# FFN 1 of a hybrid encoder layer: two more feature tiles in the seven-product scheme, with the residual's load, the norm factor, the single tiles' SwiGLU and the bias spread put elsewhere

## The chip, the cores and the metric

The kernel runs on one core of a Trainium2 chip. The metric is the device time of one execution in microseconds; of a group of runs the median counts. The profile is one execution taken by the hardware profiler. It names the engines PE (matrix multiply), PEld (its weight loads), DVE (vector), ACT (activation), POOL (GpSimd) and SP, whose queue issues most transfers. A DMA issue of an engine's queue carries a q (SPq, ACTq).

## The reference

One layer of a streaming encoder for 512 tokens of width 1024, all in float32. The part in question is the first feed-forward block:

```python
def rms_norm(x, g):
    y = x * rsqrt(mean(x * x, axis=-1, keepdims=True) + 1e-6)
    return y * g

def swiglu(x, w1, w3, w2):
    return (silu(x @ w1) * (x @ w3)) @ w2

f = swiglu(rms_norm(h, ffn1_pre_g), ffn1_w1, ffn1_w3, ffn1_w2)   # D_FF = 2816
h = h + 0.5 * rms_norm(f, ffn1_post_g)
```

Behind it come the mixer (a recurrent branch, windowed attention with a relative-position bias and sinks, gates) and a second feed-forward block of the same shape. The change touches neither; only the table of the attention's bias is prepared during FFN 1.

## The kernel before, in words

**Numbers.** A float32 factor is split into a high and a low half (`hi`, `lo`, type float32r): ACT copies the value to `hi`, DVE subtracts `hi` from the value to get `lo` (`split2`, L191 and L192; for weights of single tiles `split_to`, L156 and L157). A product is three matmuls: hi·hi, lo·hi, hi·lo.

**Tiles.** The 2816 hidden features are 22 feature tiles of 128. Tile i of `w1a` is a weight tile [128, 1024], and so is tile i of `w3a`. A *single* tile is computed by a *unit* (`unit`, `mm_feat`, L201 to L203): 8 slices of 128 channels by 3 matmuls with 512 tokens, 24 matmuls into one bank of PSUM. The transposed input stands in `uT` (high and low half).

**Pairs.** From tile NC1 on, two tiles are computed together (`Pairs`): the product of a 2x2 block of weights (two tiles by two halves of the channels) with a 2x2 block of inputs (two halves of the channels by two halves of the tokens) takes seven block products in place of eight, with sums of weight blocks (S12, S34) and of input blocks (`t1` to `t4`). A *job* is one such pair of `w1a` or of `w3a`; jobs alternate (w1a pair, w3a pair, next w1a pair), and `f` of a job is its first tile. A block product is 12 matmuls with 256 tokens (`mm_s`, L473 to L475). The products of one job, in order, by weights and inputs: a11·b11 (bank bu), s1·t1 (bank bx), [the seventh product of the job before, a22·t4], s2·t2 (added to bu), a12·b21 (bank bc), s4·b22 (added to bx), s3·t3 (added to bu). Between them ACT copies bank contents out: L551 (bu behind the first product), L554 (bx behind s1), L560 (bu behind s2), L578 (bu behind s3). A product that adds to a bank must wait until ACT has copied what stood there. DVE forms the four result blocks (L569, L574, L579), and in a `w3a` job multiplies them with the `w1a` ones (L584, L585, L598). ACT's Silu of a `w1a` job is L593 to L595 and comes behind its seventh product, in the next job.

`prep(m, i)` prepares the weights of job m: step 0 forms S12 and S34 (L518 to L521, four sums of 512 columns, on POOL or on the engine handed over), step 1 splits the first raw tile (a11, a12), step 2 splits S12 (s1, s2), step 3 S34 (s3, s4), step 4 a22 (`w22`). Inside job n stand prep(n+1, 1) to (n+1, 4), prep(n+2, 0), and the loads of job n+3 (`raws`).

**Input blocks.** `xn` is the normalized input, x·g·R: 16 operations on DVE (`norm_x`, L773), which need the spread norm factor `Rb`. The blocks b11 (from `xn`) and t1, t2 are split into slots of their own (`to_slots`: Xh, Xl); b21, b22, t3, t4 are split into `uT`, once no single unit reads it any more (`to_uT`). `sums` forms t1 to t4 by three differences on DVE (L752 to L754) and one on POOL (L751).

**Norm factor.** The residual x is loaded token-major (`h_load`, four tiles h). ACT squares and sums each (L680); `rstd4` makes 1/rms with its root on ACT (L248); DVE puts it on four diagonals (`dgs`, L686); PE multiplies these with ones (L700, bank r), which spreads the factor over all partitions; ACT copies the bank to `Rb` (L701). The single units run on x·g without the factor; it is multiplied in afterwards (`silu_mul`, L433 and L434, then Silu L435 and the product L436).

**Bias.** The relative bias comes from a small matmul of a one-hot table with the bias table (`oh`, L691), a copy (`erow`, L693) and a transfer from POOL's queue to a scratch in memory (L696), which attention reads much later.

**Order.** Every engine works off its queue strictly in the order in which the program issues. `later(n, f)` puts the issue of f at the n-th following `point`; a point stands behind every four channel slices of a unit (two a unit) and behind every block product. Buffers of [128, 1024] are 42 slots that go round: a transfer or an operation that gets a slot waits until its last user is done. SP's queue loads weight tiles in the order of `order` (`dma_to`), by need and slot. The first three units (w1a 0, w3a 0, w1a 1) run channel slice by channel slice behind the first loads; nine matmuls on zeros ahead of them warm PE up.

The part of the run in question stands in this order on PE: the first three units, unit w3a 1, the bias matmul, the factor, eight single units (w1a 2 to w3a 5), the first pair job (w1a 6 and 7).

## Time and profile before

| | |
|---|---|
| time of the runs | median 1135.27 us of 3 (1135.0 to 1135.29) |
| profiled execution | 1135.67 us, its span 1133.8 us |
| busy, share of the span | PE 99%, PEld 89%, DVE 70%, ACT 52%, POOL 31% |
| granted clock | 0.998 |
| DMA | 124.94 MB, mean 110 GB/s |

The busy time of PE counts matmuls whose ends are modelled, so a busy PE is not PE at its peak. A timeline line gives start, length, engine, line of the code, operation, output<-inputs, shapes and count; in brackets stands how long the engine was idle before it, and what ended that. A line of the waits gives engine and line, whom they waited for, us in total, times, and the longest. A line of the stretches gives from:to, its length, then for PE, PEld, DVE, ACT and POOL the busy time and the number of instructions, then the clock, the DMA share and GB/s. A line of the DMA issues gives the number, the size and the median us from issue to landing.

### The profile page before, as it was taken

To read this page: it belongs to the slowest core of one execution; us is meant where nothing else is said; L and a number is where in the kernel's file an instruction comes from. 1 tells how busy PE (TensorE), PEld (TensorE's weight loads), DVE (VectorE), ACT (ScalarE), POOL (GpSimd) and SP (SyncE) were. 2 spreads that over 40 slices of the span, in tenths; PEclk is the share of its full clock that TensorE was granted. 3 is DMA by queue.
4 is the path that set the end of the run, shared out by engine and by line. 5 is a ranking of instruction groups with operands and counts; after the bars stand their busy time and mean duration, and the time that the engine had idled before them with its cause. 6 is when DMAs were issued, how large, how long until landed. Compare 5 with 4: busy or idle time off the path is not lost.

```text
span 1133.8 us, 17339 instructions
## 1 busy us (share of the span) xinstructions
PE 1125.3 (99%) x6763; PEld 1003.5 (89%) x6763; DVE 790.1 (70%) x1181; ACT 585.2 (52%) x1042; POOL 353.8 (31%) x265
## 2 busy tenths in 40 slices
PE   9999999999999999999999999999999999999997
PEld 7889999988889987888888888889999999998886
DVE  5997889885436747695678865767899777975313
ACT  6445555574324349844655663356555555574211
POOL 0148678500000000001555643000965566700000
PEclk9999999999999999999999999999999999999999
DMA  9953223264313311234122333531323332255101
GB/s 343 157 135 112 93 95 112 76 222 151 110 56 135 144 56 57 75 95 148 56 78 90 93 95 112 185 111 38 113 94 94 112 112 76 94 197 172 40 19 56
DMA packets 36945, 124.94 MB, mean 110 GB/s; under 512 B 4416, under 2 KB 6208, under 8 KB 36864
## 3 DMA queue, kind: packets, MB, share of 16 engines
q1 hardware_dynamic: 34272, 115.15, 30.3%
q0 software_dynamic: 2448, 8.43, 4.0%
q8 instruction: 53, 0.87, 0.3%
q10 hardware_dynamic: 144, 0.26, 0.1%
q14 instruction: 28, 0.23, 0.1%
HBM read 116.50 MB, written 7.33 MB: 109 GB/s over the span
## 4 chain that ended last, share of the span: by engine, by line
PE 93%; DVE 3%; ACT 2%; issue 1%; DMA 0%; SPq 0%; DVEq 0%
PE c L475 11%; PE c L474 11%; PE c L473 11%; PE f L202 10%; PE f L201 10%; PE f L203 10%; PE acc L220 8%; PE acc L221 8%; PE acc L219 8%; PE pt L1067 1%; PE s L1031 1%; PE s L1030 1%; PE tr L310 1%; PE o L1083 1%; PE o L1084 1%
## 5 line engine op out<-in xcount | busy, mean ns | idle before, releaser
L201 PE MATMUL f<-uT,whi 128*128 128x512 f32 (+1 forms) x504 | 184.2, 365 | 0.0
L202 PE MATMUL f<-uT,wlo 128*128 128x512 f32 (+1 forms) x504 | 183.0, 363 | 0.4 <-DVE wlo L157 0.3
L203 PE MATMUL f<-uT,whi 128*128 128x512 f32 (+1 forms) x504 | 182.6, 362 | 0.0
L219 PE MATMUL acc<-whi,hT 128*128 128x512 f32 x352 | 137.1, 390 | 0.0
L220 PE MATMUL acc<-wlo,hT 128*128 128x512 f32 x352 | 137.0, 389 | 0.0
L221 PE MATMUL acc<-whi,hT 128*128 128x512 f32 x352 | 136.9, 389 | 0.0
L474 PE MATMUL c<-Xh,wlo 128*128 128x256 f32 x432 | 122.3, 283 | 0.0
L475 PE MATMUL c<-Xl,whi 128*128 128x256 f32 x432 | 122.3, 283 | 0.0
L473 PE MATMUL c<-uT,whi 128*128 128x256 f32 x432 | 122.3, 283 | 0.0
L474 PE MATMUL c<-uT,wlo 128*128 128x256 f32 x432 | 122.3, 283 | 0.0
L475 PE MATMUL c<-uT,whi 128*128 128x256 f32 x432 | 122.3, 283 | 0.0
L473 PE MATMUL c<-Xh,whi 128*128 128x256 f32 x432 | 122.3, 283 | 0.0
L192 DVE TENSOR_TENSOR wlo<-S,whi 128x1024 fp32r<-128x1024 f32 x72 | 118.2, 1642 | 3.6 <-ACT whi L191 3.2
L202 PEld LDWEIGHTS f<-uT,wlo 128*128 128x128 f32 x504 | 95.2, 189 | 15.8 <-DVE wlo L157 1.6
L201 PEld LDWEIGHTS f<-uT,whi 128*128 128x128 f32 x504 | 95.1, 189 | 15.8 <-issue 1.4
L203 PEld LDWEIGHTS f<-uT,whi 128*128 128x128 f32 x504 | 95.1, 189 | 14.8
L473 PEld LDWEIGHTS c<-Xh,whi 128*128 128x128 f32 x432 | 82.9, 192 | 0.0
L474 PEld LDWEIGHTS c<-Xh,wlo 128*128 128x128 f32 x432 | 82.9, 192 | 0.0
L473 PEld LDWEIGHTS c<-uT,whi 128*128 128x128 f32 x432 | 82.9, 192 | 0.0
L474 PEld LDWEIGHTS c<-uT,wlo 128*128 128x128 f32 x432 | 82.9, 192 | 0.0
L475 PEld LDWEIGHTS c<-uT,whi 128*128 128x128 f32 x432 | 82.9, 192 | 0.0
L475 PEld LDWEIGHTS c<-Xl,whi 128*128 128x128 f32 x432 | 82.9, 192 | 0.0
(309 smaller groups left out, 2703.8 us busy)
## 6 DMA issues: line engine op xcount, KB each, us to landing
raw_w2a<-in_w2a_dram SPq DMA_DIRECT2D x22, 512.0 KB, 3.7
raw_w1b<-in_w1b_dram SPq DMA_DIRECT2D x22, 512.0 KB, 4.2
raw_w3b<-in_w3b_dram SPq DMA_DIRECT2D x22, 512.0 KB, 4.2
raw_w2b<-in_w2b_dram SPq DMA_DIRECT2D x22, 512.0 KB, 4.1
raw_w3a<-in_w3a_dram SPq DMA_DIRECT2D x21, 512.0 KB, 4.5
raw_w1a<-in_w1a_dram SPq DMA_DIRECT2D x20, 512.0 KB, 4.5
raw_wg<-in_wg_dram SPq DMA_DIRECT2D x16, 512.0 KB, 3.7
raw_xr<-in_xr_dram SPq DMA_DIRECT2D x8, 512.0 KB, 4.7
```

Source lines behind the costliest of these rows:

```text
L192: dve.tensor_tensor(out=lo, in0=src, in1=f32(hi), op=ALU.subtract)
L201: pe.matmul(ps[:, c0:c1], wh[:, s], h_, start=k == 0, stop=False)
L202: pe.matmul(ps[:, c0:c1], wl[:, s], h_, start=False, stop=False)
L203: pe.matmul(ps[:, c0:c1], wh[:, s], l_, start=False, stop=k == KT - 1)
L219: pe.matmul(acc[n], x[:, 0, c], wh[:, s], start=first, stop=False)
L220: pe.matmul(acc[n], x[:, 0, c], wl[:, s], start=False, stop=False)
L221: pe.matmul(acc[n], x[:, 1, c], wh[:, s], start=False, stop=last)
L310: pe.transpose(ps[:, k * P : (k + 1) * P], hg[:, kk * P : (kk + 1) * P], ident)
L473: pe.matmul(ps, wh[:, s], xh, start=first, stop=False, skip_group_check=True)
L474: pe.matmul(ps, wl[:, s], xh, start=False, stop=False, skip_group_check=True)
L475: pe.matmul(ps, wh[:, s], xl, start=False, stop=k == 3, skip_group_check=True)
L1030: pe.matmul(o, lq, KS[g][:, 0, k0 : k0 + n], start=True, stop=False)
```

## The change

NC1 goes from 6 to 4: tiles 4 and 5 are computed as a pair (two jobs) and no longer as four units. With that, the surrounding work is placed anew.

- The four residual tiles are loaded ahead of the third next weight tile (w1a 2) instead of behind it, and only w3a 1 is split ahead of the squares.
- The factor's matmuls and the copy to `Rb` are issued in the middle of unit w3a 1 (`later(1, factor)`) instead of behind it.
- The banks of the eight single units are copied out raw by ACT (`keep`, two to a slot). Their SwiGLU (`swiglu_late`: two multiplies by `Rb` on DVE, Silu on ACT, a multiply on DVE) runs in jobs 1 to 4, one tile each, behind the first product. `hid.f` has its first four places reserved for them.
- `norm_x`, the differences (`t_sums`) and the splits of b11, t1, t2 are spread over the points of five units instead of nine; the first preparation of job 0 comes behind them (its sums on DVE, as before), and of job 1 only step 0 is issued ahead.
- The load of Silu's activation table (a Silu of `tiny`) moves from behind the root to behind the last bank copy, ahead of b21's split.
- The bias tables are loaded in job 3 and spread in job 5.

```diff
@@ the first loads
-    dma_to(NS + 2)
+    dma_to(NS + 1)
     h_load([a["x"][t * P : (t + 1) * P, :] for t in range(NT)])
+    dma_to(NS + 2)
     hid, X1 = Hidden(), {}
+    hid.f += [None] * NC1
...
     dma_one(pairs_a.k0 + 1)
+    dma_to(NS + 4)
...
-    oh = slot([N_BUCKETS, NREL + 1 + N_HEADS], name="oh")
-    pool.dma_start(out=oh[:, : NREL + 1], in_=a["onehot"])
-    pool.dma_start(out=oh[:, NREL + 1 :], in_=a["rel_bias"])
@@ behind the first three units
-    split_to(NS + 2)
+    split_to(NS + 1)
...
-    r, q = rstd4(s4)
-    act.activation(tiny, q, AF.Silu)
+    r, _ = rstd4(s4)
...
-    pairs_a.prep(0, 0, dve)
-    ps.append(unit("w3a", 1))
-    pse = bank("e")
-    pe.matmul(pse[:N_HEADS, : NREL + 1], oh[:, NREL + 1 :], oh[:, : NREL + 1], start=True, stop=True)
...
-    act.activation(Rb, psr, AF.Copy)
-    pairs_a.prep(0, 1)
-    hid.f += [silu_mul(ps[0], ps[1], Rb), silu_mul(ps[2], ps[3], Rb)]
-    pairs_a.prep(0, 2)
-    later(1, lambda: pairs_a.prep(0, 3))
-    later(2, lambda: pairs_a.prep(0, 4))
+    def factor():
+        psr = bank("r")
+        for t in range(NT):
+            pe.matmul(psr[:, t * P : (t + 1) * P], ones, dgs[:, t, :], start=True, stop=True)
+        act.activation(Rb, psr, AF.Copy)
+    later(1, factor)
+    def bias_in():
+        oh.append(slot([N_BUCKETS, NREL + 1 + N_HEADS], name="oh"))
+        pool.dma_start(out=oh[0][:, : NREL + 1], in_=a["onehot"])
+        pool.dma_start(out=oh[0][:, NREL + 1 :], in_=a["rel_bias"])
+    def bias_spread():
+        pse = bank("e")
+        t = oh.pop()
+        pe.matmul(pse[:N_HEADS, : NREL + 1], t[:, NREL + 1 :], t[:, : NREL + 1], start=True, stop=True)
+        erow = slot([N_HEADS, NREL + 1], name="erow")
+        act.activation(erow, pse[:N_HEADS, : NREL + 1], AF.Copy)
...
@@ the single units and the input blocks
-    def swiglu_units(na, nb, f0, f1, hid, R=None):
-        for f in range(f0, f1):
-            p1, p3 = unit(na, f), unit(nb, f)
-            later(1, lambda p1=p1, p3=p3: hid.f.append(silu_mul(p1, p3, R)))
+    def keep(f, e, ps):
+        if f not in raw:
+            raw[f] = slot([P, 2, SEQ], name="raw")
+        act.activation(raw[f][:, e, :], ps, AF.Copy)
+    def swiglu_late(f):
+        t = raw.pop(f)
+        for e in range(2):
+            dve.tensor_tensor(out=t[:, e, :], in0=t[:, e, :], in1=Rb, op=ALU.mult)
+        act.activation(t[:, 0, :], t[:, 0, :], AF.Silu)
+        dve.tensor_tensor(out=t[:, 1, :], in0=t[:, 1, :], in1=t[:, 0, :], op=ALU.mult)
+        hid.f[f] = t[:, 1, :]
+    def single(nm, i, ahead):
+        w = get(nm, i, ahead=ahead)
+        ps = bank("f")
+        mm_feat(ps, w)
+        return ps
...
-    for k in range(KT):
-        later(2 + k // 2, lambda k=k: norm_x(k))
-    later(6, lambda: xts.clear())
-    later(6, lambda: tn.extend(sums(xn)))
-    later(7, lambda: X1.update(b11=to_slots(xn[0, 0])))
-    later(9, lambda: X1.update(t1=to_slots(tn[0])))
-    later(11, lambda: X1.update(t2=to_slots(tn[1])))
-    end = 2 * 2 * (NC1 - 2)
-    for i, at_ in enumerate((end - 5, end - 2, end - 1)):
-        later(at_, lambda i=i: pairs_a.prep(1, i))
-    swiglu_units("w1a", "w3a", 2, NC1, hid, Rb)
+    def t_sums(n):
+        t = slot([P, 4, 256], name="T")
+        tn[n] = t
+        if n == 2:
+            pool.tensor_tensor(out=t, in0=xn[1, 1], in1=xn[0, 1], op=ALU.subtract)
+            return
+        p, q = ((xn[0, 1], xn[0, 0]), (xn[1, 1], tn.get(0)), None, (xn[1, 0], tn.get(1)))[n]
+        dve.tensor_tensor(out=t, in0=p, in1=q, op=ALU.subtract)
+    for k in range(4):
+        later(1, lambda k=k: norm_x(k))
+    later(3, lambda: X1.update(b11=to_slots(xn[0, 0])))
+    later(3, lambda: t_sums(0))
+    for k in range(4, KT):
+        later(3 + (k > 5), lambda k=k: norm_x(k))
+    later(4, lambda: xts.clear())
+    later(5, lambda: X1.update(t1=to_slots(tn[0])))
+    later(5, lambda: t_sums(1))
+    later(6, lambda: t_sums(2))
+    later(6, lambda: t_sums(3))
+    later(6, lambda: X1.update(t2=to_slots(tn[1])))
+    later(7, lambda: pairs_a.prep(0, 0, dve))
+    later(7, lambda: pairs_a.prep(0, 1))
+    later(8, lambda: pairs_a.prep(0, 2))
+    later(9, lambda: pairs_a.prep(0, 3))
+    later(10, lambda: pairs_a.prep(1, 0))
+    later(10, lambda: pairs_a.prep(0, 4))
+    later(7, lambda: dma_to(pairs_a.k0 + 4))
+    ps.append(single("w3a", 1, 1))
+    for n, p_ in enumerate(ps):
+        keep(n // 2, n % 2, p_)
+    p1 = single("w1a", 2, 1)
+    later(1, lambda: keep(2, 0, p1))
+    p3 = single("w3a", 2, 1)
+    later(1, lambda: keep(2, 1, p3))
+    p1_ = single("w1a", 3, 1)
+    later(1, lambda: keep(3, 0, p1_))
+    p3_ = single("w3a", 3, 0)
     point(True)
+    keep(3, 1, p3_)
+    act.activation(tiny, tiny, AF.Silu)
     X1["b21"] = to_uT(xn[1, 0], 1, 0)
     late = {
...
+        (3, 1): [bias_in],
+        (5, 3): [bias_spread],
     }
+    for f in range(NC1):
+        late.setdefault((f + 1, 1), []).append(lambda f=f: swiglu_late(f))
...
-NC1 = 6
+NC1 = 4
```

Job numbers count from the first pair job of the kernel in hand: job 0 is w1a 6 and 7 before, w1a 4 and 5 after.

More of the change, by code (lines that the diff above doesn't have):

```diff
@@ L639, in hybrid_layer @@
         load_x(2 * kp + 1)
+    dma_to(NS + 1)
+    h_load([a["x"][t * P : (t + 1) * P, :] for t in range(NT)])
     dma_to(NS + 2)
-    h_load([a["x"][t * P : (t + 1) * P, :] for t in range(NT)])
     hid, X1 = Hidden(), {}
+    hid.f += [None] * NC1
     pairs_a = Pairs("w1a", "w3a", NC1, X1, hid)
@@ L686, in hybrid_layer @@
         dve.tensor_scalar(out=dgs[:, t, :], in0=ident, scalar1=r[:, t : t + 1], scalar2=NEWT, op0=ALU.mult, op1=ALU.mult)
-    pairs_a.prep(0, 0, dve)
-    ps.append(unit("w3a", 1))
-    pse = bank("e")
-    pe.matmul(pse[:N_HEADS, : NREL + 1], oh[:, NREL + 1 :], oh[:, : NREL + 1], start=True, stop=True)
-    erow = slot([N_HEADS, NREL + 1], name="erow")
-    act.activation(erow, pse[:N_HEADS, : NREL + 1], AF.Copy)
-    scr = tc.dram_tile([N_HEADS, P, NREL], F32, name="bias_scr")
-    ev = erow[:, :NREL]
-    pool.dma_start(out=scr, in_=bass.AP(tensor=ev.tensor, offset=ev.offset, ap=[ev.ap[0], [0, P], ev.ap[1]]))
-    Rb = slot([P, SEQ], name="Rb")
-    psr = bank("r")
-    for t in range(NT):
-        pe.matmul(psr[:, t * P : (t + 1) * P], ones, dgs[:, t, :], start=True, stop=True)
-    act.activation(Rb, psr, AF.Copy)
-    pairs_a.prep(0, 1)
-    hid.f += [silu_mul(ps[0], ps[1], Rb), silu_mul(ps[2], ps[3], Rb)]
-    pairs_a.prep(0, 2)
-    later(1, lambda: pairs_a.prep(0, 3))
-    later(2, lambda: pairs_a.prep(0, 4))
+    Rb = slot([P, SEQ], name="Rb")
+    def factor():
[4 more added lines that the diff above has]
+    later(1, factor)
+    scr = tc.dram_tile([N_HEADS, P, NREL], F32, name="bias_scr")
+    oh = []
+    def bias_in():
[8 more added lines that the diff above has]
+        act.activation(erow, pse[:N_HEADS, : NREL + 1], AF.Copy)
+        ev = erow[:, :NREL]
+        pool.dma_start(out=scr, in_=bass.AP(tensor=ev.tensor, offset=ev.offset, ap=[ev.ap[0], [0, P], ev.ap[1]]))
     def softplus():
@@ L734, in softplus @@
                     scalar1=0.5, scalar2=None, op0=ALU.mult)
-    def swiglu_units(na, nb, f0, f1, hid, R=None):
-        for f in range(f0, f1):
-            p1, p3 = unit(na, f), unit(nb, f)
-            later(1, lambda p1=p1, p3=p3: hid.f.append(silu_mul(p1, p3, R)))
+    raw = {}
+    def keep(f, e, ps):
[14 more added lines that the diff above has]
+        return ps
     def uview(hh, th):
@@ L746, in pair_view @@
         return lambda e, k: p[e][:, k, :]
-    def sums(xf):
-        t = [slot([P, 4, 256], name="T") for _ in range(4)]
-        pool.tensor_tensor(out=t[2], in0=xf[1, 1], in1=xf[0, 1], op=ALU.subtract)
-        dve.tensor_tensor(out=t[0], in0=xf[0, 1], in1=xf[0, 0], op=ALU.subtract)
-        dve.tensor_tensor(out=t[1], in0=xf[1, 1], in1=t[0], op=ALU.subtract)
-        dve.tensor_tensor(out=t[3], in0=xf[1, 0], in1=t[1], op=ALU.subtract)
-        return t
     def to_slots(src):
@@ L765, in to_uT @@
         return uview(hh, th)
-    xn, tn = {(hh, th): slot([P, 4, 256], name="xn") for hh in range(2) for th in range(2)}, []
+    xn, tn = {(hh, th): slot([P, 4, 256], name="xn") for hh in range(2) for th in range(2)}, {}
     def norm_x(k):
```

## The prediction

> **What bounds the kernel now.** I read the page's totals and its chain first, then the waits of PE for the whole run, then the timelines of PE, DVE, POOL and ACT from the start to the second pair job.

> ```profile
> span 1133.8 us, 17339 instructions
> PE 1125.3 (99%) x6763; PEld 1003.5 (89%) x6763; DVE 790.1 (70%) x1181; ACT 585.2 (52%) x1042; POOL 353.8 (31%) x265
> PE 93%; DVE 3%; ACT 2%; issue 1%; DMA 0%; SPq 0%; DVEq 0%
> PE f L202 <- DVE wlo L157: 0.3, 1, 0.3
> ```

> PE is never let go: the last line is its longest wait behind the start. So the change wins exactly the PE work it removes, and loses every time something comes late. All it moves lies ahead of the sixth pair job. There the order of work is this (start, length):

> ```profile
> 22.71 0.39 PE L201 MATMUL f<-uT,whi 128*128 128x512 f32 x1
> 27.92 0.39 PE L203 MATMUL f<-uT,whi 128*128 128x512 f32 x1
> 28.98 1.16 PE L700 MATMUL r<-dgs,ones 128*128 128x128 f32 x8
> 29.90 0.48 PE L201 MATMUL f<-uT,whi 128*128 128x512 f32 x1
> 57.22 0.39 PE L201 MATMUL f<-uT,whi 128*128 128x512 f32 x1
> 57.90 0.50 PE L202 MATMUL f<-uT,wlo 128*128 128x512 f32 x1 [0.30 <-DVE wlo L157]
> 74.13 0.28 PE L473 MATMUL c<-Xh,whi 128*128 128x256 f32 x1
> 84.40 0.38 ACT L551 ACTIVATE ct<-c 128x256 f32<-128x256 f32 x1 [0.54 <-PE c L475]
> 94.48 0.39 ACT L551 ACTIVATE ct<-c 128x256 f32<-128x256 f32 x1 [0.53 <-PE c L475]
> 30.00:74.10 44.10, 43.80 (x194) 35.95 (x193) 41.40 (x52) 18.47 (x23) 10.75 (x6) 1.00 0.78 125
> ```

> The first two lines are matmuls 1 and 24 of unit w3a1: 5.21 us over 23 steps, 0.2265 us each, 5.44 a unit. ACT's copy L551 comes once a job: 10.08 us. The last line is the stretch of eight single units: of 44.1 us PE is busy 43.8 and DVE 41.4. DVE is nearly full there, and the change shortens this very stretch.

> **What decides: DVE and POOL block each other.** POOL's rows, then DVE's:

> ```profile
> 50.10 2.40 POOL L751 TENSOR_TENSOR T<-xn,xn 128x1024 f32<-128x1024 f32 x1 [18.73 <-DVE xn L773]
> 67.63 1.62 POOL L519 TENSOR_TENSOR S<-S,raw_w3a 128x512 f32<-128x512 f32 x1
> 69.32 2.16 POOL L520 TENSOR_TENSOR S<-raw_w3a,S 128x512 f32<-128x512 f32 x1
> 71.44 2.27 POOL L521 TENSOR_TENSOR S<-raw_w3a,raw_w3a 128x512 f32<-128x512 f32 x1
> 50.45 0.70 DVE L434 TENSOR_TENSOR sw<-f,Rb 128x512 f32<-128x512 f32 x1
> 51.25 1.81 DVE L436 TENSOR_TENSOR sw<-sw 128x512 f32<-128x512 f32 x1
> 56.63 1.22 DVE L157 TENSOR_TENSOR wlo<-raw_w3a,whi 128x1024 fp32r<-128x1024 f32 x1
> 68.17 2.16 DVE L192 TENSOR_TENSOR wlo<-raw_w3a,whi 128x1024 fp32r<-128x1024 f32 x1
> 70.37 2.19 DVE L192 TENSOR_TENSOR wlo<-S,whi 128x1024 fp32r<-128x1024 f32 x1
> ```

> The ends interlock: POOL 69.25, DVE 70.33, POOL 71.48, DVE 72.56, POOL 73.71. They take strict turns, 1.08 us for a 1024-wide DVE split, 1.15 for a 512-wide POOL sum; alone the split is 1.22, and 1.13 from one to the next where they follow each other. L436 ends at 53.06, 0.56 behind POOL's 52.50. L434, with one input from PSUM, was not slowed. So each POOL sum costs a waiting DVE queue its whole length.

> **The change, part by part.**

> *Tiles 4 and 5 paired.* Four units go, 4 x 5.44 = 21.74; two jobs come, 20.16: −1.6 us. The late wait at 57.9 goes: 57.90−57.22−0.23 = −0.45. The factor matmuls and the bias matmul stay on PE, elsewhere. Without any new wait −2.0.

> *Residual ahead.* SP now loads the four h tiles before w1a2.

> ```profile
> 17.11 1.06 ACT L156 ACTIVATE whi<-raw_w3a 128x1024 fp32r<-128x1024 f32 x1 [1.31 <-DMA raw_w3a<-in_w3a_dram]
> 18.37 1.06 ACT L156 ACTIVATE whi<-raw_w1a 128x1024 fp32r<-128x1024 f32 x1 [0.19 <-DMA raw_w1a<-in_w1a_dram]
> 24.96 1.28 ACT L683 ACT_TABLE_LOAD   x1
> 26.25 0.21 ACT L683 ACTIVATE tiny<-r 128x4 f32<-128x4 f32 x1
> 25.64 0.88 DVE L686 TENSOR_SCALAR dgs<-ident,r 128x128 f32<-128x128 f32 x4
> 30.18 0.60 ACT L701 ACTIVATE Rb<-r 128x512 f32<-128x512 f32 x1
> ```

> Transfers land 1.26 apart, so the squares and dgs come one place earlier: ready at 26.52−1.25 = 25.27. PE asks for them in mid-unit, at 22.71+12x0.2265 = 25.43: no wait (0 to +0.5). w1a2 lands near 17.1+5x1.25 = 23.4 and is used at 29.07: free.

> *Factor inside w3a1.* Its 0.92 (28.98 to 29.90) only moves. From its start to the end of Rb took 1.80, so Rb is ready at 27.23 instead of 30.78. Units then start at 29.07 (w1a2), 34.51, 39.95 and 45.39 (w3a3); the first job could start at 50.83.

> *DVE's list in those units.*

> ```profile
> 43.96 3.26 DVE L773 SCALAR_TENSOR_TENSOR xn<-xt,vec,Rb 128x256 f32<-128x256 f32 x8
> ```

> From 27.25: eight norm_x (3.17) to 30.4; ACT copies w3a1's bank behind the unit's end and only then writes w3a2's high half, done near 30.9; split w3a2, Xl of b11 and T0 at 1.13 each, to 34.35; eight norm_x to 37.5. Now xn is whole, and POOL's T2 is released, with S of job 1 (four sums) queued behind it; its raw tiles were asked for at 27 and 32. DVE still has six lines ahead of PE's need: w1a3, Xl of t1, T1, T3, Xl of t2, w3a3. Taking turns: w1a3 38.65, T2 40.95 (2.3), Xl 42.05, sum 43.2, T1 44.3, sum 45.45, T3 46.55, sum 47.7, Xl 48.8, sum 49.95, w3a3 51.05. PE needs w3a3's low half at 45.39+0.23 = 45.62. **PE waits 5.4 us**; the first job starts near 56.3, not 50.83. Bounds: 0 (without turns the list ends at 37.5+6x1.13 = 44.3) and 6 us.

> *Last bank copied, then the activation table.*

> ```profile
> 74.10 1.06 ACT L191 ACTIVATE uT<-xn 128x1024 fp32r<-128x1024 f32 x1 [0.27 <-PE f L202]
> 75.82 0.39 ACT L551 ACTIVATE ct<-c 128x256 f32<-128x256 f32 x1 [0.66 <-PE c L475]
> raw_w1a<-in_w1a_dram SPq DMA_DIRECT2D x20, 512.0 KB, 4.5
> ```

> A job's product is 12 of its 84 matmuls, 1.44 us; L551 starts 0.25 behind its end. Counted from PE's end T of w3a3, ACT has keep(3,1) from 0.25 (0.60, as the Rb row), the table 1.28, tiny 0.21, b21's high half 1.06, and only then L551 (0.39) of job 0, which frees the bank that product 3 adds to: 3.8. PE is there at 2.88. **+0.9** (0 to 1.3).

> *Job 0 splits more.* Before, the first two splits of job 1 were done ahead. Now DVE has b21, b22, t3, a11, t4 and s12 from 3.5 on, and between them POOL's four sums of job 2, whose raw tiles wait for w3a3's slots and land near 4.5 (the 4.5 of the last row): 6x1.1+4x1.15 = 11.2, so s12 is ready at 14.7. Job 1's second product needs it from its second matmul on and ends at 16.0; without waits it would end at 8.64+2.88 = 11.5 (job 0 runs six products, its seventh comes in job 1). 4.5 late, the 0.9 included: **+3.6** (0 to 4.5).

> *SwiGLU of single tiles in jobs 1 to 4.* Its Silu stands on ACT between L551 and L554 and waits for a DVE multiply queued behind the next job's last split. Behind Silu wait L554, which frees the bank of product s4, then three activations, a split and L560, which frees that of s3. Job 1 on DVE: two PSUM adds 15.3, s34 16.4, L579 16.7, sum 17.85, w22 18.4, sum 19.55, multiply 20.1; on ACT Silu 20.8, L554 21.05. PE, three products behind 16.0, is there at 20.4: 0.6 late. L560 ends at 23.45, PE is there at 22.5: 1.0 more, and job 2 starts at 24.95. In job 2 the multiply stands behind L579, L584, L585 and w22 with three sums between, 33.2; L554 ends at 34.1, PE is there at 32.1: 2.0. Going on so, job 3 loses nothing, job 4 0.45: **+4.05** (0 to 7: my turns may err by a sum or two a job).

> *Bias.* Its loads and its spread are three DMA issues in POOL's queue, near 1 us each, with sums behind them:

> ```profile
> 30.34 1.03 POOL L696 DMA_DIRECT2D bias_scr<-erow  x1 [27.64 <-ACT erow L693]
> 96.85 1.67 POOL L518 TENSOR_TENSOR S<-raw_w1a 128x512 f32<-128x512 f32 x1 [2.43 <-DVE cc L585]
> 117.31 1.29 POOL L518 TENSOR_TENSOR S<-raw_w1a 128x512 f32<-128x512 f32 x1 [4.83 <-DVE w L192]
> 109.63 1.70 DVE L192 TENSOR_TENSOR wlo<-raw_w1a,whi 128x1024 fp32r<-128x1024 f32 x1 [3.51 <-ACT whi L191]
> ```

> POOL waits 2.4 and 4.8 us ahead of such a group: 0 (to +1).

> Sum: −2.0+5.4+0.9+3.6+4.05 = +11.95. The profiled execution took 1135.67 (1.9 around its span), 0.4 over the median of 1135.27: 1147.6 against itself, 1147.2 against the median, so **1147**. A change under 0.2% (2.3 us) would not count.

> **Rivals.**

> *No turns at the stated place* (POOL's T2 and sums arrive late or yield): DVE is done at 44.3, job 0 loses only 0.9: −2.0+0.9, 1134.2, not slower. It decides if POOL takes under 1.3 us out of the list between 37.5 and 45.6. For it: DVE alone fits. Against: every meeting quoted above took turns. 0.10.

> *Only the wait at w3a3, jobs absorb the rest*: −2.0+5.4+0.9 = +4.3, 1139.6. For it: in steady jobs PE waits for none. Against: DVE's spare there is a gap like the 3.51 of the last row, one in two jobs, while each SwiGLU adds three DVE multiplies (1.8), and job 0 starts late. 0.20.

> *The clock falls during the wait.* At the start nine matmuls took longer:

> ```profile
> 1.45 4.21 PE L625 MATMUL w<-warm 128*128 128x512 f32 x9 [1.45 <-DVE tiny L629]
> ```

> That is 0.468 each, 2.2 us lost over 4.2. If a PE idle for 5.4 us falls back so, 1149.4. No PE wait here is long enough to show it. [...] 0.22.

> *The forecast*, without such a fall: 0.48.

> **How the numbers follow.** The range takes in the two rivals on the slow side and the upper ends of the job terms (+3 us): 1138.5 to 1152. Outside lies the first rival and a remainder of larger errors. Faster needs no waits at all and no table cost, even then −2.0 is under 0.2%: 0.04. Same is the rest of the first rival: 0.08. Slower: 0.88.

> **What would show it.** In the changed kernel's timeline: r near 25.4; Rb near 27; POOL's T2 near 38.7; w3a3's split ending near 51 and PE waiting for it about 5 us, which should be the longest wait of PE; the first pair matmul near 56; PE waits on ACT in jobs 0 to 2 behind the table load and behind Silu; from job 5 a job again every 10.08. Wrong, if PE's waits for DVE stay under 1 us, or if POOL's sums run beside DVE's splits without lengthening them.

## The result: 1161.81 us, slower by 2.4%, and the profile after

The changed kernel took 1161.81 us (median of five runs, 1161.35 to 1162.8), the kernel before 1135.27 beside it. The ratio is 1.0236 (interval 1.0221 to 1.0251), 26.5 us more. The forecast was 1147, with a range up to 1152: the direction was right, the size less than half of what came (11.7 of 26.5 us).

From the page of the changed kernel, its totals and chain:

```profile
span 1159.9 us, 17537 instructions
PE 1130.7 (97%) x6835; PEld 1010.5 (87%) x6835; DVE 809.9 (70%) x1188; ACT 593.4 (51%) x1063; POOL 370.9 (32%) x273
PE 80%; ACT 2%; DVE 1%; issue 0%; DVEq 0%
```

PE's share of the span fell from 99% to 97%. The largest of its waits in the changed kernel, over the whole run and then one by one, in order of time:

```profile
PE c L474 <- DVE wlo L192: 7.9, 8, 2.7
PE c L473 <- ACT ct L560: 6.2, 1, 6.2
PE f L202 <- DVE wlo L157: 3.0, 1, 3.0
PE c L473 <- ACT ct L554: 2.0, 1, 2.0
```

```profile
48.55 0.50 PE L202 MATMUL f<-uT,wlo 128*128 128x512 f32 x1 [2.97 <-DVE wlo L157]
58.66 0.39 PE L473 MATMUL c<-Xh,whi 128*128 128x256 f32 x1 [1.16 <-ACT ct L551]
69.78 0.39 PE L474 MATMUL c<-Xh,wlo 128*128 128x256 f32 x1 [2.75 <-DVE wlo L192]
89.46 0.39 PE L473 MATMUL c<-uT,whi 128*128 128x256 f32 x1 [2.02 <-ACT ct L554]
161.01 0.58 PE L473 MATMUL c<-uT,whi 128*128 128x256 f32 x1 [6.16 <-ACT ct L560]
```

The first four stand where the forecast put its waits. The fifth is not in it. How the loss builds up is read at ACT's copy L551, which comes once a job. The same two jobs, first before, then after:

```profile
124.72 0.38 ACT L551 ACTIVATE ct<-c 128x256 f32<-128x256 f32 x1 [0.54 <-PE c L475]
175.12 0.38 ACT L551 ACTIVATE ct<-c 128x256 f32<-128x256 f32 x1 [0.54 <-PE c L475]
```

```profile
137.61 0.38 ACT L551 ACTIVATE ct<-c 128x256 f32<-128x256 f32 x1 [0.54 <-PE c L475]
201.25 0.38 ACT L551 ACTIVATE ct<-c 128x256 f32<-128x256 f32 x1 [0.54 <-PE c L475]
```

At the first of them the changed kernel is 12.9 us late, where the forecast had 12. Between them it loses another 13.2 us, and from there to the end nothing. The place of these 13 us, first in the waits of SP's queue, then in the timelines of POOL, SP and ACT, last as a stretch of ten us:

```profile
SPq L141 <- DMA bias_scr<-erow: 33.9, 1, 33.9
```

```profile
122.47 1.03 POOL L711 DMA_DIRECT2D bias_scr<-erow  x1 [7.28 <-ACT erow L709]
155.84 0.82 SPq L141 DMA_DIRECT2D raw_w3a<-in_w3a_dram  x2
159.63 1.06 ACT L191 ACTIVATE whi<-raw_w3a 128x1024 fp32r<-128x1024 f32 x1 [10.12 <-DMA raw_w3a<-in_w3a_dram]
161.00 2.08 POOL L518 TENSOR_TENSOR S<-raw_w3a 128x512 f32<-128x512 f32 x1 [20.69 <-DMA raw_w3a<-in_w3a_dram]
```

```profile
153.00:163.00 10.00, 3.84 (x25) 3.64 (x24) 1.23 (x1) 1.33 (x2) 2.00 (x1) 0.83 0.76 248
```

The bias spread was issued at 122.47 and takes 33.3 us from issue to landing, to 155.8. Its source `erow` stands in one of the 42 slots that go round. SP's next load waits 33.9 us for the spread to end; a load has no other tie to the spread than this slot. SP's queue works in order, so between the load issued at 121.6 and 155.84 no weight tile is asked for. The tiles in store last until about 150. Then ACT's split waits 10.1 us for its tile, L560 stands behind that split, and PE waits 6.16 us. Behind it PE ran at half rate for some 5 us; the clock of the last line is 0.83. Four shorter waits follow up to 191 us, 3.4 us in all (the longest 1.70), three of them for VectorE's splits: from 173 to 193 us VectorE is never idle, and it seems that the late tiles give it and POOL their work all at once.

### The profile page after: what moved, and what is told of

Same layout as the page of the kernel before. It is cut to its first block, busy times and chain, and to the rows that moved or that the text cites. A ratio compares the mean times of both kernels' runs of the same rounds, so it can differ in the third digit from the quotient of the medians.

```text
span 1159.9 us, 17537 instructions
## 1 busy us (share of the span) xinstructions
PE 1130.7 (97%) x6835; PEld 1010.5 (87%) x6835; DVE 809.9 (70%) x1188; ACT 593.4 (51%) x1063; POOL 370.9 (32%) x273
## 4 chain that ended last, share of the span: by engine, by line
PE 80%; ACT 2%; DVE 1%; issue 0%; DVEq 0%
PE f L202 9%; PE f L201 9%; PE f L203 9%; PE acc L220 8%; PE acc L219 8%; PE acc L221 8%; PE c L474 8%; PE c L475 8%; PE c L473 8%; PE pt L1113 1%; PE s L1077 1%; PE s L1076 1%; PE tr L310 1%; PE o L1129 1%; PE o L1130 1%; PE r L921 0%
## 5 line engine op out<-in xcount | busy, mean ns | idle before, releaser
L202 PE MATMUL f<-uT,wlo 128*128 128x512 f32 (+1 forms) x472 | 170.8, 362 | 3.0 <-DVE wlo L157 3.0
L201 PE MATMUL f<-uT,whi 128*128 128x512 f32 (+1 forms) x472 | 171.9, 364 | 0.0
L203 PE MATMUL f<-uT,whi 128*128 128x512 f32 (+1 forms) x472 | 170.4, 361 | 0.0
L474 PE MATMUL c<-Xh,wlo 128*128 128x256 f32 x456 | 130.8, 287 | 7.9 <-DVE wlo L192 7.9
L473 PE MATMUL c<-uT,whi 128*128 128x256 f32 x456 | 130.3, 286 | 8.2 <-ACT ct L560 6.2
L473 PE MATMUL c<-Xh,whi 128*128 128x256 f32 x456 | 130.1, 285 | 1.2 <-ACT ct L551 1.2
L475 PE MATMUL c<-Xl,whi 128*128 128x256 f32 x456 | 129.9, 285 | 0.0
L475 PE MATMUL c<-uT,whi 128*128 128x256 f32 x456 | 129.8, 285 | 0.0
L474 PE MATMUL c<-uT,wlo 128*128 128x256 f32 x456 | 129.8, 285 | 0.0
L192 DVE TENSOR_TENSOR wlo<-S,whi 128x1024 fp32r<-128x1024 f32 x76 | 122.6, 1614 | 7.3 <-ACT whi L191 6.9
L202 PEld LDWEIGHTS f<-uT,wlo 128*128 128x128 f32 x472 | 89.2, 189 | 17.2 <-DVE wlo L157 4.3
L201 PEld LDWEIGHTS f<-uT,whi 128*128 128x128 f32 x472 | 89.2, 189 | 14.5 <-issue 1.4
L203 PEld LDWEIGHTS f<-uT,whi 128*128 128x128 f32 x472 | 89.1, 189 | 13.5
L474 PEld LDWEIGHTS c<-Xh,wlo 128*128 128x128 f32 x456 | 88.3, 194 | 9.6 <-DVE wlo L192 9.6
L473 PEld LDWEIGHTS c<-uT,whi 128*128 128x128 f32 x456 | 88.1, 193 | 9.4 <-ACT ct L560 6.4
L473 PEld LDWEIGHTS c<-Xh,whi 128*128 128x128 f32 x456 | 88.4, 194 | 1.4 <-ACT ct L551 1.4
L475 PEld LDWEIGHTS c<-Xl,whi 128*128 128x128 f32 x456 | 88.3, 194 | 0.0
L475 PEld LDWEIGHTS c<-uT,whi 128*128 128x128 f32 x456 | 88.2, 193 | 0.0
L474 PEld LDWEIGHTS c<-uT,wlo 128*128 128x128 f32 x456 | 88.2, 193 | 0.0
## 6 DMA issues: line engine op xcount, KB each, us to landing
raw_w2a<-in_w2a_dram SPq DMA_DIRECT2D x22, 512.0 KB, 4.0
raw_w1b<-in_w1b_dram SPq DMA_DIRECT2D x22, 512.0 KB, 4.1
raw_w3b<-in_w3b_dram SPq DMA_DIRECT2D x22, 512.0 KB, 4.1
raw_w2b<-in_w2b_dram SPq DMA_DIRECT2D x22, 512.0 KB, 4.3
raw_w3a<-in_w3a_dram SPq DMA_DIRECT2D x21, 512.0 KB, 4.5
raw_w1a<-in_w1a_dram SPq DMA_DIRECT2D x20, 512.0 KB, 4.3
raw_wg<-in_wg_dram SPq DMA_DIRECT2D x16, 512.0 KB, 3.7
raw_xr<-in_xr_dram SPq DMA_DIRECT2D x8, 512.0 KB, 3.9
```

The costliest lines, as they stand in the source:

```text
L192: dve.tensor_tensor(out=lo, in0=src, in1=f32(hi), op=ALU.subtract)
L201: pe.matmul(ps[:, c0:c1], wh[:, s], h_, start=k == 0, stop=False)
L202: pe.matmul(ps[:, c0:c1], wl[:, s], h_, start=False, stop=False)
L203: pe.matmul(ps[:, c0:c1], wh[:, s], l_, start=False, stop=k == KT - 1)
L473: pe.matmul(ps, wh[:, s], xh, start=first, stop=False, skip_group_check=True)
L474: pe.matmul(ps, wl[:, s], xh, start=False, stop=False, skip_group_check=True)
```

## The experiments

### The place of the bias spread

Four runs move only the bias. The first two:

```diff
@@ the changed kernel: bias at its old place
     pool.memset(ones, 1.0)
+    bias_in()
...
     ps.append(single("w3a", 1, 1))
+    bias_spread()
...
-        (3, 1): [bias_in],
-        (5, 3): [bias_spread],
@@ the kernel before: bias at the new place
-    oh = slot([N_BUCKETS, NREL + 1 + N_HEADS], name="oh")
...
+        (1, 1): [bias_in],
+        (3, 3): [bias_spread],
```

> The changed kernel with one part undone: the bias table's small loads stand at the start again and its product and spread behind the single unit of w3a 1, as in the kernel before. Theory A (the spread's 33 us transfer keeps the pair jobs' tile loads back, and that is the half of the loss that the prediction priced at 0): about 1148 us, 13 below the changed kernel; the wait of 6.2 us at L560 near 161 us and the half clock behind it are gone, and raw_w3a lands in time throughout. Rival B (the transfer is hidden wherever it stands, the second half of the loss comes from the waits that job 0 hands on): 1160 to 1162 us, with waits of several us still between 150 and 195 us. Both expect the waits up to 137 us as they were: 3.0 at the split of w3a 3, 1.2 at L551, some 4 at the splits of the jobs 0 and 1, 2.0 at L554.

> The kernel before with only the bias moved: small loads at w1a 8's job, product and spread at w1a 9's, at the very places (by feature tile) that the changed kernel uses. Theory A (the transfer collides with the jobs' loads, without any help from the other edits): about 1148 us, 13 above the kernel before, with a wait of some 6 us a few jobs behind the spread and a lower granted clock there. Rival B (the transfer is free there; the loss needs the late job 0): 1134 to 1137 us. Rival C (both are needed, since the changed kernel's jobs have less slack left): between, 1138 to 1143 us.

Measured: 1151.66 us (ratio 1.0145, 1.0128 to 1.0162) and 1150.4 us (1.0132, 1.0117 to 1.0147). The early bias takes 10.2 us off the changed kernel, where theory A had 13. The bias alone, moved in the kernel before, costs 15 us, where theory A had 13: none of the other edits is needed for it. But what both expectations have in mind, tiles' loads that run slowly beside the transfer, is not what the trace shows first. In the kernel before with the late bias it is POOL that meets the slot (timelines of POOL and PE, then a stretch):

```profile
109.41 1.03 POOL L715 DMA_DIRECT2D bias_scr<-erow  x1 [4.30 <-ACT erow L713]
143.56 1.26 POOL L520 TENSOR_TENSOR S<-raw_w1a,S 128x512 f32<-128x512 f32 x1 [22.73 <-DMA bias_scr<-erow]
147.45 0.58 PE L473 MATMUL c<-uT,w 128*128 128x256 f32 x1 [11.43 <-ACT ct L578]
```

```profile
143.00:153.00 10.00, 5.55 (x26) 5.55 (x27) 5.84 (x5) 3.36 (x7) 9.29 (x7) 0.50 0.37 150
```

A sum waits 22.7 us for the spread, and so for `erow`'s slot; ACT's split of that sum, L578 behind it and PE follow. At L578 PE waits 11.4 us, and then runs the stretch at clock 0.50. Besides, SP's loads that were issued during the spread landed after 17.1 us in the median (five of them, 6.9 to 21.4), and after 3.7 behind it: a second effect, which the early place has too (in the kernel before, three loads issued during the spread landed after 13.1 us in the median). PE's only long wait here is the one behind the slot.

The other two put the bias where the tiles' rate is low, between the units of xr and of wg, about 100 us ahead of its first reader:

```diff
         xr_ps[i] = unit("xr", i)
+        if i == 5:
+            bias_in()
+    bias_spread()
```

> The changed kernel with the bias moved behind the pair jobs and w2a, into the stage of xr and wg, where the slices of the span near 410 to 460 us show 55 GB/s; the table is first read at 547 us. Nothing else differs. Theory A (the spread costs what its neighbours lose, so here nothing; the rest of the change costs what stood up to 137 us): 1147 to 1149 us, with the waits up to 92 us as in the changed kernel and none behind them. Rival B (any place collides, since the single units too need 512 KB in some 5 us): 1152 us or more, with PE waits between 410 and 460 us.

> The kernel before with only the bias moved to the same place in the stage of wg. Theory A (the transfer was hidden where it stood, beside the single units, and is hidden here): 1134.5 to 1136 us, no change. Rival B (the transfer held up something in the prelude too): 1132 to 1134 us. Rival C (it collides in the wg stage): 1138 us or more.

Measured: 1149.75 us (1.0122, 1.0106 to 1.0137) and 1135.16 us (1.0000, 0.9991 to 1.0008). There the spread costs nothing in either kernel; no instruction waits for it until its reader. So the late bias is worth 1161.81−1149.75 = 12.1 us in the changed kernel and 1150.4−1135.16 = 15.2 us in the one before. The old place may not be free in the changed kernel: it is 1.9 us above the place at wg, but the two intervals overlap (in that run the shortened prelude has the spread beside it, and an ACT split waited 2.1 us for the slot).

### Cutting the transfer

```diff
-        pool.dma_start(out=scr, in_=bass.AP(tensor=ev.tensor, offset=ev.offset, ap=[ev.ap[0], [0, P], ev.ap[1]]))
+        ev = oh[0][2 * i : 2 * i + 2, :NREL]
+        pool.dma_start(out=scr[2 * i : 2 * i + 2], in_=bass.AP(tensor=ev.tensor, offset=ev.offset, ap=[ev.ap[0], [0, P], ev.ap[1]]))
@@ and in a further run, in place of these two lines
+        ev = oh[0][:, :NREL]
+        pool.dma_start(out=scr[:, 16 * i : 16 * i + 16], in_=bass.AP(tensor=ev.tensor, offset=ev.offset, ap=[ev.ap[0], [0, 16], ev.ap[1]]))
```

> The changed kernel with its late bias, but the spread cut into eight transfers of two heads each (383 KB), one per job from w1a 9's on. Theory A (one transfer of 33 us occupies all the DMA engines for three jobs, and each job needs 1 MB of tiles in 10 us with only two jobs' worth ahead; a piece takes some 4 us, so that every job still has 6 us for its tiles): the wait of 6.2 us near 161 us and its half clock are gone, 1147 to 1150 us, at or a little below the run with the bias early. Rival B (what hurts is the sum of bytes, or POOL's queue standing behind the transfers): 1156 us or more, the waits spread over eight jobs.

> The kernel before with the bias moved as in the earlier run of this kind (1150.4 us), but cut into the same eight transfers. Theory A: the whole loss of 15 us goes, 1134 to 1137 us; the PE wait of 11.4 us behind L578 is gone. Rival B (bytes, not the length of the one transfer): 1143 us or more.

> The changed kernel with the spread at w1a 9's job and the seven behind it, in eight pieces as in the run that took 1183.6 us, but each piece writes all 16 heads for 16 of the 128 repetitions, so that it reads 16 partitions and not 2. Theory A (a transfer from 2 partitions is slow, 25 us for 383 KB, because few DMA engines carry it, and the tiles' loads wait for these engines; from 16 partitions a piece takes some 4 us and hinders one load a little): a piece lands in 4 to 6 us and the time is 1147 to 1152 us, below the changed kernel's 1161.8. Rival B (any transfer of the software queue beside the tiles' loads costs its whole length): 1160 us or more.

Measured: 1183.57 us (1.0423), 1159.7 us (1.0216) and 1150.12 us (1.0132, 1.0118 to 1.0146). The first two expectations failed badly, the third held for theory A. The two cuts in the changed kernel, first two rows of `erow` a piece, then all 16 rows: the pieces among the DMA issues, and how long SP's loads between 124 and 190 us took to land:

```profile
bias_scr<-erow POOLq DMA_DIRECT2D x8, 383.0 KB, 29.3
```

```profile
DMA to landing us min/median/max: 5.0/19.0/24.5
```

```profile
bias_scr<-erow POOLq DMA_DIRECT2D x8, 383.0 KB, 5.7
```

```profile
DMA to landing us min/median/max: 3.5/4.4/5.9
```

Same bytes, same jobs, same number of issues: 29.3 us a piece against 5.7 (25.3 with two rows in the kernel before). Theory A's few DMA engines are not shown: no run here shows which engines carry a piece, nor what the loads beside it wait for. In short pieces from all rows the late place is 0.4 us above the place at wg, which is within the noise. Neither the bytes nor the late place as such cost 12 us. In both cuts the program holds `erow` until its last piece is issued, and no instruction waited for the slot; so what lies between the two cuts, 33.5 us, comes without any wait for the slot.

In the changed kernel itself it is the slot: SP's wait of 33.9 us names it, and as SP asked for nothing during the spread, no load ran slowly beside it (the five loads from 120.8 to 157 us landed after 3.6 to 5.4 us). What is not shown is how much of the 12 us a free slot would have saved, since loads beside the spread are slow too (17.1 and 13.1 us in the median, in the kernel before); `erow` in a buffer of its own was not tried.

### POOL's sums and the SwiGLU, one at a time

```diff
@@ the sums
-    later(6, lambda: t_sums(2))
...
-    later(10, lambda: pairs_a.prep(1, 0))
     later(10, lambda: pairs_a.prep(0, 4))
+    later(10, lambda: t_sums(2))
+    later(10, lambda: pairs_a.prep(1, 0, dve))
...
-            pool.tensor_tensor(out=t, in0=xn[1, 1], in1=xn[0, 1], op=ALU.subtract)
+            dve.tensor_tensor(out=t, in0=xn[1, 1], in1=xn[0, 1], op=ALU.subtract)
@@ the SwiGLU
-        late.setdefault((f + 1, 1), []).append(lambda f=f: swiglu_late(f))
+        late.setdefault((f + 1, 1), []).append(lambda f=f: scale_raw(f))
+        late.setdefault((f + 1, 3), []).append(lambda f=f: swiglu_late(f))
```

> The first kernel of this call (bias early) with POOL kept out of the prelude: the activations' sum T2 and the four sums of job 1's weights go to VectorE, behind job 0's last split. Theory A (VectorE and POOL take turns, so POOL's five instructions stretch VectorE's): the split of w3a 3 takes 1.2 us and not 2.3 and ends some 3 us earlier, the wait of 3.0 us in front of w3a 3 is gone, and the time is 3 to 5 us below the first kernel's, some 1144 us. Rival B (VectorE has simply too much to do: 3.6 us more work of its own costs what the turns cost): within 1 us of the first kernel, the waits moved from w3a 3 into the jobs 0 and 1.

> The first kernel of this call (bias early) with the late SwiGLU cut in two: VectorE's two products with the norm factor stay at the job's first point, Silu and the last product move to its third, so that ScalarE has no Silu that waits for VectorE between L551 and L554. Theory A (Silu waits 6 to 8 us for VectorE's products and L554 stands behind it): the wait of 2.0 us for L554 in job 2 is gone, the jobs 1 to 4 gain 2 to 4 us together, some 1145 us. Rival B (VectorE is late in these jobs anyway, Silu only shows it): the wait returns at L560 or at the splits, within 1 us of the first kernel.

Both with the early bias: 1150.36 and 1151.47 us, 1.3 and 0.2 below the run with the early bias alone, neither clear of the noise. For the SwiGLU rival B held: PE's wait for L554 went from 4.7 us to none, its waits at L474 rose from 3.7 to 7.3. For the sums the early spread spoiled the reading: VectorE, which now needed job 1's tiles in time for their sums, met a late one (3.69 us), and PE waited 4.58 us. So both were repeated with the bias at wg, the SwiGLU now at the jobs 5, 7, 9 and 11 (`2 * f + 5` for `f + 1`):

> The run with the bias at wg (1149.75 us) and besides only T2 and the sums of job 1 on VectorE, behind job 0's last split. Theory A (POOL's five instructions beside VectorE's are what costs 3.0 us at w3a 3 and some 3 us at the splits of job 1): 1143 to 1145 us; unlike the earlier run of this edit, the tiles are there in time, so no wait of 4.6 us for the sums. Rival B (the SwiGLU in the jobs 1 to 4 takes up what is gained): 1147 us or more.

> The run with the bias at wg (1149.75 us) and besides only the late SwiGLU in two parts at the jobs 5, 7, 9 and 11. Theory A (the predicted term: Silu in the jobs 1 to 4 and its three products on a full VectorE cost about 4 us, and the new place costs some of it back, as the three waits of 0.8, 0.5 and 0.5 us of the run with the repairs show): 1145 to 1148 us. Rival B (the SwiGLU pushes the backlog of job 0 through four jobs, and without it VectorE catches up in one): 1140 to 1144 us.

Measured: 1145.69 us (1.0089, 1.0074 to 1.0104) and 1145.75 us (1.0089, 1.0072 to 1.0106): 4.1 and 4.0 us below 1149.75. VectorE's list ahead of w3a 3, and POOL's, in the changed kernel:

```profile
37.50 5.49 POOL L794 TENSOR_TENSOR T<-xn,xn 128x1024 f32<-128x1024 f32 x1 [36.05 <-DVE xn L786]
37.24 1.22 DVE L157 TENSOR_TENSOR wlo<-raw_w1a,whi 128x1024 fp32r<-128x1024 f32 x1
38.38 1.21 DVE L192 TENSOR_TENSOR Xl<-T,Xh 128x1024 fp32r<-128x1024 f32 x1
39.51 4.56 DVE L797 TENSOR_TENSOR T<-xn,T 128x1024 f32<-128x1024 f32 x2
43.99 2.31 DVE L192 TENSOR_TENSOR Xl<-T,Xh 128x1024 fp32r<-128x1024 f32 x1
46.22 2.28 DVE L157 TENSOR_TENSOR wlo<-raw_w3a,whi 128x1024 fp32r<-128x1024 f32 x1
```

and with the sums on VectorE:

```profile
39.24 2.55 DVE L797 TENSOR_TENSOR T<-xn,T 128x1024 f32<-128x1024 f32 x2
41.70 1.22 DVE L192 TENSOR_TENSOR Xl<-T,Xh 128x1024 fp32r<-128x1024 f32 x1
42.84 1.22 DVE L157 TENSOR_TENSOR wlo<-raw_w3a,whi 128x1024 fp32r<-128x1024 f32 x1
```

POOL's T2 was released at 37.5 and stood 5.49 us, where 2.40 is what it took before. VectorE did a split, an Xl and part of L797 at their own length first; only then the two alternate, and VectorE's last two lines take 2.31 and 2.28 us in place of 1.22. Without POOL the split of w3a 3 ends at 44.06, in time, and the wait of 2.97 us is gone. That is not the whole 4.1 us, and not all of it is waits: in the two profiled runs PE's waits between 31 and 240 us are 8.2 us against 10.0, spread over ten places, and the run with the bias at wg has three stretches of 3.4 us at half rate where this one has none (the last section says what decides that). The SwiGLU run lost its waits between 75 and 140 us and gained three at its new place (0.99, 0.46 and 0.47 us).

One run stands aside: the late SwiGLU on top of the two-row pieces.

> The run with the spread in pieces, and besides only the late SwiGLU in two parts and at the jobs 5, 7, 9, 11. Theory A (in the jobs 1 to 4 VectorE is full, and the three products of a SwiGLU, beside POOL's sums, are the last straw; from job 5 on it has room): the waits at L554 and those at the splits after 80 us are gone, 4 to 6 us below the run with the pieces alone. Rival B (the backlog of job 0 is the cause, the SwiGLU only carries it): within 1.5 us of it.

It took 1171.34 us, 12.2 below the pieces alone and not 4 to 6. With loads as slow as that the two runs differ in too many waits to say why, so it does not measure the SwiGLU.

### All repairs together

Besides the sums on VectorE and the SwiGLU at the jobs 5 to 11, these load Silu's table early again and put job 2's sums on VectorE:

```diff
-    act.activation(tiny, tiny, AF.Silu)
...
-    r, _ = rstd4(s4)
+    r, q = rstd4(s4)
+    act.activation(tiny, q, AF.Silu)
...
-                self.prep(n + 2, 0)
+                self.prep(n + 2, 0, dve if self.na == 'w1a' and n < 1 else None)
```

> The changed kernel with every suspect mended at once: spread in eight pieces, Silu's table loaded behind the norm factor, T2 and the sums of the jobs 1 and 2 on VectorE, the late SwiGLU in two parts and at the jobs 5, 7, 9 and 11 in place of 1 to 4. Theory A (four units become two jobs and save about 2 us; what else the change costs is waits for VectorE in the jobs 0 to 4 and the spread): 1134 to 1138 us, PE waits under 4 us in all up to 200 us and the granted clock at 1.00 there. Rival B (job 0's own splits of the activations and the weights are more than VectorE can do in 10 us, so the jobs 0 and 1 wait and the clock falls anyway): 1140 to 1145 us.

With the two-row pieces 1161.75 us, far above both ranges expected; up to the spread it was on time (L551 of w3a 6's job at 83.90 us, before 84.40). With the pieces replaced by the one transfer at wg:

> The run with all repairs, with its pieces replaced by the one transfer in the stage of wg. In the run with the repairs L551 of the job of w3a 6 stood at 83.90 us, 0.5 us ahead of the same job before (84.40), while the pieces came behind it. Theory A (the pairing itself gains half a microsecond to a microsecond once VectorE's load is spread and the transfer is out of the way): 1133.5 to 1135 us, within 0.2% of the kernel before. Rival B (waits at the new places of the late SwiGLU, jobs 5 to 11, or the transfer in the wg stage): 1137 to 1142 us.

1139.35 us (1.0037, 1.0025 to 1.0050), 10.4 below 1149.75; the two single repairs together gave 8.1; the other 2.3 come with the table and job 2's sums, which were not tried alone. Of what is left, rival B names the smaller part: waits of 0.80, 0.46 and 0.47 us behind the late SwiGLU. The larger is a wait of 1.78 us near 72 us, for job 2's first split, with 3.4 us at half rate behind it.

The SwiGLU's place was then tried at the other jobs, in three parts:

```diff
+        n = 4 + 2 * f
+        late.setdefault((n, 1), []).append(lambda f=f: scale_raw(f, 0))
+        late.setdefault((n, 3), []).append(lambda f=f: scale_raw(f, 1))
+        late.setdefault((n + 1, 1), []).append(lambda f=f: silu(f))
+        late.setdefault((n + 2, 1), []).append(lambda f=f: gate(f))
```

> The run with all repairs and the bias at wg (1139.35 us), its late SwiGLU spread further: the two products with the norm factor at two points of the jobs 4, 6, 8 and 10 (w1a, where VectorE has no products of the pair to form), Silu one job and the last product two jobs behind. Theory A (the waits of 0.80, 0.46 and 0.47 us in the jobs 8, 10 and 12, and the 0.7 to 1 us that each of these jobs was longer, came from three products in one job): 1134.5 to 1136.5 us, no PE wait behind 80 us. Rival B (VectorE's backlog from POOL's turns is as long in every job): 1138 to 1140 us.

> As the run before, but the sums of job 2 stay with POOL. Theory A (four more instructions on VectorE in job 1, beside POOL's four for job 3, made the wait of 1.78 us at job 2's first split near 72 us; on POOL they lie beside the splits of job 0 and cost as much there): within 1 us of the run before. Rival B (POOL's turns are cheaper than VectorE's own work): 1 to 2 us below it.

1143.93 and 1146.9 us: worse, with waits up to 2.2 us, and both expectations were misses. I had taken the w1a jobs for the lighter ones, because the pair's products belong to the w3a jobs; but VectorE does them a job later, since it runs behind. Its timeline shows where it is idle, here in an odd job of the first of the two runs:

```profile
106.70 0.68 DVE L192 TENSOR_TENSOR w<-raw_w3a,w 128x512 fp32r<-128x512 f32 x1
109.94 1.33 DVE L192 TENSOR_TENSOR wlo<-raw_w1a,whi 128x1024 fp32r<-128x1024 f32 x1 [2.56 <-ACT whi L191]
```

By the second run job 2's four sums cost 3.0 us more on POOL than on VectorE in this kernel. The last two runs put every product at the first point of the odd jobs, and the second of them job 3's sums on VectorE too:

```diff
-        n = 4 + 2 * f
+        n = 5 + 2 * f
...
-        late.setdefault((n, 3), []).append(lambda f=f: scale_raw(f, 1))
+        late.setdefault((n, 1), []).append(lambda f=f: scale_raw(f, 1))
@@ the second
-                self.prep(n + 2, 0, dve if self.na == 'w1a' and n < 1 else None)
+                self.prep(n + 2, 0, dve if self.na == 'w1a' and n < 2 else None)
```

> The run with all repairs and the bias at wg (1139.35 us), with the late SwiGLU's products all at the first point of the odd jobs, where VectorE's trace showed an idle stretch of 2.6 us (5, 7, 9, 11: two products with the norm factor; 7, 9, 11, 13: the last product; Silu at the first point of the even jobs between). Theory A (the last product at the third point, 1.8 us beside POOL, made the splits late that the waits of 0.80, 0.46 and 0.47 us stand for): those waits and the 0.8 to 1.1 us by which four jobs were longer go, 1135 to 1136.5 us. Rival B (VectorE is full in any job): 1138 us or more.

> As the run before, and the sums of job 3 on VectorE too, so that POOL has nothing to do beside VectorE's sums of job 2. Theory A (VectorE's four sums of job 2 took 5.8 us in place of 2.8 beside POOL's for job 3): the wait of 1.78 us near 72 us and any half clock behind it go, 1 to 3 us below the run before, 1133 to 1135 us. Rival B (POOL takes up job 4's sums in that place): within 0.5 us of it.

1136.25 us (1.0011, 1.0002 to 1.0020) and 1135.41 us (1.0002, 0.9992 to 1.0011). The first is theory A's time. The second is 0.8 below it, less than theory A's 1 to 3; the wait of 1.78 us near 72 us is gone as expected, but one of 0.84 stands at 81.6. PE's waits of the second, from 20 to 240 us:

```profile
PE c L474 <- DVE wlo L192: 0.8, 1, 0.8
PE c L475 <- DVE uT L192: 0.7, 1, 0.7
```

Two waits, 1.6 us, are left of the 21 us of PE's waits in the changed kernel, and the pairing then is as fast as the kernel before, not faster. At the last w3a job L551 stands at 224.36 us; in the kernel before with the bias at wg it stands at 224.22. The 2.0 us that the forecast puts on the pairing are there, and the two waits, with what PE loses around them, take them back: the two jobs that hold them are 1.0 and 1.1 us longer than the same jobs elsewhere.

## Why the prediction was wrong, step by step

**Failed: "Bias ... 0 (to +1)".** The step counted what POOL issues and looked for room in POOL's queue. It did not ask how long the transfer keeps its source, nor what stands in the ring of slots behind it. Measured: 12.1 us in the changed kernel, 15.2 alone in the kernel before. So two of its signs failed as well: the longest wait of PE was not the one at w3a 3 but the 6.16 us at L560, and from job 5 on a job did not come every 10.08 us. The trace before had the duration (33.3 us from issue to landing) and the prelude had the cover: eight single units in which nobody needed that slot. With a price of 0 the whole forecast was for the other edits, and for those it came out near: 1149.75 where the bias is out of the way, against 1147.

**Partly luck: that 1149.75 is so near 1147.** In the profiled run with the bias at wg PE's waits up to 240 us are 10.0 us, where the forecast's are 13.95. Three stretches of 3.4 us at half rate, for which the forecast had nothing, cost about 5 us more (an estimate: half of 3 x 3.41). The two errors nearly cancel.

**Right in kind, 2.4 us too large: the wait at w3a 3.** "Taking turns: ... w3a3 51.05" and a wait of 5.4 us. The split ended at 48.50 and PE waited 2.97. The turns were not strict from the start: T2 was let in after some 3 us (an estimate: 5.49 less the 2.40 of before), so POOL had fewer instructions between VectorE's. That VectorE and POOL stretch each other, and that w3a 3 is where it shows, the runs bear out (the 2.97 us are gone without POOL).

**Right in place and near in size: table, job 0, SwiGLU.** Table 0.9, measured 1.16 (0.55 in the run with the bias at wg). Job 0 and the first splits of job 1: 3.6, measured 0.56+2.75, and behind it some 1.5 us lost to half rate. SwiGLU: 2.0 at L554 of job 2, measured 2.02; 4.05 for all, and 4.0 less when it moves away. That the last two agree is again partly luck: the moved run pays 1.9 us of waits at the new place, and its profile has one stretch of half rate in place of three.

**The pairing itself: −2.0.** The last run fits it: with two jobs 2.1 us longer than the others it ties.

**Rivals.** No turns: refuted by the doubled splits (2.31 and 2.28 us against 1.22). Only the wait at w3a 3: refuted by the 2.75 and 2.02 later on. The clock rival was right that the rate can fall at w3a 3, and its wait of 5.4 us is more than it takes: with the bias at wg the rate fell behind 2.99 us there. In the changed kernel's profile it stayed full behind the 2.97 us at w3a 3, and fell at 70.91 us behind the wait that ends at 69.8, and at 159.66 us within the one that ends at 161. The forecast of a wait of 5.4 us without any fall did not fit together: wherever such a wait lies, at least 2.7 us of it (half of 5.4) fall into one window of 3.41, and 1.78 were enough in the traces of the last section.

## What to carry to other kernels

A transfer that reads from a rotating buffer holds that buffer until it lands: here for 33.3 us, and SP's next load waited 33.9 us for it. Before moving it, take its time from issue to landing, and see which instruction gets the buffer next and whose queue stands behind it. A large transfer belongs where neither its buffer nor the DMA engines are wanted (their share was 0.96 to 1.00 from 123 to 153 us of the changed kernel; at wg the spread cost nothing, beside the jobs 12.1 and 15.2 us). If it is cut, it should be cut so that every piece still spans all its rows, as here: 5.7 us a piece against 29.3. Work moved from one engine's idle time to another stage is to be placed by the engine's timeline in that stage, not by which job the work belongs to.

## What was not expected of the hardware

A wait shorter than 3 us can halve PE's rate for 3.4 us, and the same wait need not. In the run with the Silu behind (bias early), a wait of 2.13 us:

```profile
48.98 0.80 PE L202 MATMUL f<-uT,wlo 128*128 128x512 f32 x1 [2.13 <-DVE wlo L157]
50.00 0.63 PE L201 MATMUL f<-uT,whi 128*128 128x512 f32 x1
50.43 0.63 PE L202 MATMUL f<-uT,wlo 128*128 128x512 f32 x1
50.85 0.63 PE L203 MATMUL f<-uT,whi 128*128 128x512 f32 x1
```

The matmuls follow at 0.43 in place of 0.227. Behind the wait of 2.97 us at the same place of the changed kernel they did not slow down; behind 2.99 us, in the run with the bias at wg, they did. Two runs with all repairs had the same wait of 1.78 us near 72 us, and only one of them slowed down.

```profile
69.95:73.36 3.41, 1.63 (x14) 1.43 (x13) 3.41 (x4) 1.85 (x3) 1.20 (x1) 1.00 0.00 0
73.36:76.77 3.41, 3.41 (x19) 3.41 (x18) 3.41 (x7) 0.39 (x2) 1.19 (x1) 0.50 0.00 0
```

```profile
68.41:71.82 3.41, 2.21 (x19) 2.00 (x17) 3.41 (x3) 1.66 (x3) 2.85 (x2) 1.00 0.18 72
71.82:75.23 3.41, 2.83 (x23) 2.83 (x24) 3.41 (x6) 0.57 (x2) 0.00 (x0) 1.00 0.00 0
75.23:78.64 3.41, 3.41 (x31) 3.41 (x30) 3.41 (x5) 1.63 (x4) 2.87 (x2) 1.00 0.00 0
```

The waits at w3a 3 go the same way, first in the changed kernel, then with the bias at wg:

```profile
43.60:47.02 3.42, 1.98 (x9) 1.31 (x7) 3.42 (x3) 0.60 (x2) 3.34 (x2) 1.00 0.00 0
47.02:50.43 3.41, 1.88 (x8) 1.57 (x9) 3.38 (x3) 0.00 (x0) 3.33 (x3) 1.00 0.00 0
50.43:53.84 3.41, 3.41 (x17) 2.83 (x16) 3.31 (x4) 1.58 (x2) 0.92 (x1) 1.00 0.00 0
```

```profile
46.43:49.84 3.41, 1.37 (x6) 1.15 (x7) 3.41 (x2) 0.00 (x0) 3.33 (x3) 1.00 0.00 0
49.84:53.26 3.42, 3.42 (x10) 2.67 (x9) 3.28 (x5) 1.09 (x2) 1.41 (x1) 0.50 0.00 0
```

In all 20 traces, from 25 to 300 us, every window at full rate in which PE was idle for 1.78 us or more (42 of them) was followed by one at half rate, and none in which it was idle for 1.73 us or less. The limit lies a little above half the window; as the ends of matmuls are modelled, it is no sharper than that. So a window need not be idle as a whole: 1.78 us of its 3.41 were enough.

For reading these runs this means that a wait of 1.8 to 3.5 us (up to twice 1.73) costs some 1.5 us more or not, by where it happens to lie (an estimate from half of 3.41 us). Single runs that differ by that much need not differ in their waits.
